# Other constants in the time estimate by which a trace-time scheduler orders a two-layer hybrid transformer

## The chip, the cores and the metric

The kernel runs on one core of a Trainium2 chip. The metric is the device time of one execution in microseconds (us); lower is better. All times come from the hardware profiler or from timed runs.

## The reference

Two layers work on 256 latent tokens and 256 context tokens of width 1024. The second layer gives out the latent tokens alone. In short:

```python
for l in range(DEPTH):                                   # DEPTH = 2
    h_lat = modulate(x, m_lat[0][:, None], m_lat[1][:, None])
    h_ctx = modulate(xc, m_ctx[0], m_ctx[1])
    # token_mixer: one input projection (1024 to N_IN), then
    #   A) differential attention, 4 heads of 2 x 64, rotary positions on latent tokens
    #   B) bidirectional chunked gated delta rule, 4 heads of 128, short convolution on q, k, v
    #   y = (g_a * (ya @ w_pa) + g_b * (yb @ w_pb)) @ w_o
    y_lat, y_ctx = token_mixer(h_lat, h_ctx, ...)
    x = layer_norm(alpha * x + m_lat[2][:, None] * y_lat, ln1_g[l], ln1_b[l])
    # moe_ffn: 16 SwiGLU experts of width 512, router, top-2 inside one of 4 groups
    y = moe_ffn(tokens, router_w, router_b, w_exp1[l], w_exp3[l], w_exp2[l])
    x = layer_norm(alpha * x + m_lat[5][:, None] * y_lat, ln2_g[l], ln2_b[l])
```

All inputs are float32.

## The kernel before, in words

The Python program does not write its instructions in the order in which they run. It describes some eighty strands per layer (generators such as `conv_worker`, `build`, `invert`, `scan`, `attend`, `gates`, `merge`, `out_proj`, `moe_in`, `route`, `expert_up`). Each strand hands operations to a `Scheduler` while the program is being built; the scheduler picks one operation after the other and issues it, so each engine's instruction queue is the order of those picks. On the chip every engine then goes through its queue in that order, and waits on semaphores where an operand is not there yet.

A pick goes by an estimate. Each operation carries a list of (engine, estimated us, function that issues it). `plan` works out when the operation could start: the later of the time at which its engine is free and the time at which its operands are ready plus `LAT` (0.13 us; PE's instructions 0.1 us more). For an operation that ScalarE or VectorE could do, such as `cpy`, it takes the engine with the earlier estimated end, VectorE with a penalty of 1.0 us. A PE operation is counted twice as long where the PE columns counted in the tick before stayed under `COLUMNS`; `emit` counts those columns from the operation's own estimate. `run` then takes, among all strands' next operations, those that could start within 0.05 us of the earliest, and of these the one with the lowest priority number (table `PRIO`, by layer and strand). Strands of negative priority (`moe_in` and `route`) also keep others off an engine: another strand's operation is only taken there if it would end by 0.1 us after the urgent one could start. `emit` books the engine as busy for the estimate, and the result as ready at the same moment.

```python
cand = [(s,) + self.plan(s.q[0]) for s in self.strands if s.q]
...
ok = [c for c in cand if c[0].prio < 0 or c[2] + c[1][1] < due.get(c[1][0], 1e9) + 0.1]
...
    first = min(c[2] for c in ok) + 0.05
    best = min((c for c in ok if c[2] <= first), key=lambda c: c[0].prio)
```

The helpers that record operations hold the constants: `mm` (matmul, line 451 of the trace), `mm_beside` (several experts' matmuls side by side, line 463), `tr` (transpose, line 468), `dve` and `acte` (the formulas for VectorE and ScalarE), `act` (line 480), `cpy` (line 485), `tt` (line 489), `neg` (line 494), `vtr`, `ts` (lines 504 and 506), `affine` (line 511), `stt` (line 518), `vcopy` (line 522), `vset` (line 526), `reduce` (line 529). `mm` and `tr` are PE operations. Because all strands share these helpers, a line of the trace is a kind of operation and not a place in the algorithm; the place is told by the time.

Memory is scheduled too: pages of 128 x 2048 float32 (20 of them), smaller tiles, and 8 PSUM banks are taken and given back by strands, and a table of limits by phase (`LIMITS`) says how many pages the weights may hold. The weights stream in a fixed order (`PLAN`, then each layer's experts), through SP's queue, 1 MB at a time. Weights of the projections are split by `split` into a rounded part and a rest (ScalarE, then VectorE), so that three fast matmuls (`mm3`) replace one full float32 matmul. The experts of rank 2 and higher are loaded by the ranks that the router's counts give, so their loads cannot start before `route` has written `eidi`; those of rank 0 and 1 can be loaded ahead.

Where the steps of the mixer lie in the algorithm: `build` sets up the chunk matrices of the delta rule, `invert` and `double` invert them (small matmuls of 32 x 32, 32 x 64 and 64 x 64), `scan` goes through the chunks, `residual_in` loads the rows that `moe_in` needs (the gate row `gr` by `mod_rows` from `m_dram`), `out_proj` is the last large matmul of a mixer, `moe_in` makes the residual and the norm, `route` the ranking.

Of the kernel before, what the change touches and what calls it, by code (L numbers as in the profile page):

```python
# [12 lines left out]
F32R = mybir.dt.float32r  # L13
BF = mybir.dt.bfloat16
I32 = mybir.dt.int32
AF = mybir.ActivationFunctionType
OP = mybir.AluOpType
# [111 lines left out]
def width(ap):  # L129
    return math.prod(ap.shape[1:])  # L130
# [275 lines left out]
def tile_kernel(ctx, tc, x_in, c_in, ctx_in, cctx_in, mod_w, mod_b, w_in, conv_w, lam_q1, lam_k1, lam_q2,  # L406
# [3 lines left out]
    V, S, G, PE = nc.vector, nc.scalar, nc.gpsimd, nc.tensor  # L410
# [18 lines left out]
    SC = Scheduler(make)  # L429
# [7 lines left out]
    def in_psum(ap):  # L437
        return SC.phys.get(ap.tensor.name, "")[:1] == ("bank",)

    def aps(*xs):  # L440
        return [x for x in xs if x is not None and not isinstance(x, (int, float))]

    def mm(o, a, b, start, stop, beside=False):
        n = max(width(b), 16)
        t = n / 2400 if b.dtype == BF or (b.dtype == F32R and n >= 256) else n / 600
        if beside:
            t = 0.0
        elif b.dtype == F32:
            t = max(t, width(a) / 1200)
        SC.rec([("PE", max(t, 0.022) + 0.003,  # L450
                 lambda: PE.matmul(o, a, b, start=start, stop=stop, skip_group_check=True))], [o], [a, b])  # L451

    def mm3(o, a, b, start, stop):

        mm(o, a[0], b[0], start, False)
        mm(o, a[0], b[1], False, False)
        mm(o, a[1], b[0], False, stop)
# [7 lines left out]

    def tr(o, a, idn=None):
        idn = ident if idn is None else idn
        SC.rec([("PE", 0.11, lambda: PE.transpose(o, a, idn))], [o], [a])  # L468

    def dve(n, ps, r=1.0):  # L470
        return 0.065 + n * 0.00104 * (1.0 if ps else r) + (0.06 if ps else 0.0)

    def acte(n, ps):
        return (0.05 if ps else 0.093) + n * 0.000834

    def act(o, a, f=AF.Copy, bias=0.0, scale=1.0, accum_out=None):
        if f == AF.Copy and (not isinstance(bias, float) or not isinstance(scale, float)):
            f = AF.Identity
        k = {} if accum_out is None else {"accum_out": accum_out}
        SC.rec([("ACT", acte(width(o), in_psum(a)), lambda: S.activation(o, a, f, bias=bias, scale=scale, **k))],  # L480
               aps(o, accum_out), aps(a, bias, scale))

    def cpy(o, a):

        SC.rec([("ACT", acte(width(o), in_psum(a)), lambda: S.activation(o, a, AF.Copy, bias=0.0, scale=1.0)),  # L485
                ("DVE", dve(width(o), in_psum(a), 0.5), lambda: V.tensor_copy(o, a))], [o], [a], pen=1.0)

    def tt(o, a, b, op, e="DVE"):
        opts = [("DVE", dve(width(o), in_psum(a) or in_psum(b)), lambda: V.tensor_tensor(out=o, in0=a, in1=b, op=op)),  # L489
                ("POOL", 0.1 + width(o) * 0.00218, lambda: G.tensor_tensor(out=o, in0=a, in1=b, op=op))]  # L490
        SC.rec({"DVE": opts[:1], "POOL": opts[1:], "ANY": opts}[e], [o], [a, b])

    def neg(o, a):
        SC.rec([("ACT", acte(width(o), in_psum(a)), lambda: S.activation(o, a, AF.Copy, bias=0.0, scale=-1.0)),
                ("DVE", dve(width(o), in_psum(a), 0.5), lambda: V.tensor_scalar(o, a, -1.0, None, op0=OP.mult))],
               [o], [a], pen=1.0)

    def vtr(o, a):
# [3 lines left out]
    def ts(o, a, s1, op0, s2=None, op1=None):  # L502
        if op1 is None:
            f = lambda: V.tensor_scalar(o, a, s1, None, op0=op0)  # L504
        else:
            f = lambda: V.tensor_scalar(o, a, s1, s2, op0=op0, op1=op1)  # L506
        SC.rec([("DVE", dve(width(o), in_psum(a), 0.5), f)], [o], aps(a, s1, s2))

    def affine(o, a, s, b):

        SC.rec([("ACT", acte(width(o), in_psum(a)), lambda: S.activation(o, a, AF.Identity, bias=b, scale=s)),
                ("DVE", dve(width(o), in_psum(a), 0.5),
                 lambda: V.tensor_scalar(o, a, s, b, op0=OP.mult, op1=OP.add))], [o], [a, s, b])

    def stt(o, a, s, b, op0, op1, accum_out=None):
# [3 lines left out]
               aps(o, accum_out), aps(a, s, b))  # L519

    def vcopy(o, a):
        SC.rec([("DVE", dve(width(o), in_psum(a), 0.5), lambda: V.tensor_copy(o, a))], [o], [a])

    def vset(o, x, e="DVE"):
        eng = V if e == "DVE" else G
# [17 lines left out]
    def split(h, lo, a):  # L543

        cpy(h, a)
        tt(lo, a, h.bitcast(F32), OP.subtract)

    def rsqrt(y, a, scale, z):

        ts(a, a, scale, OP.mult, EPS, OP.add)  # L550
        ts(y.bitcast(I32), a.bitcast(I32), -0.5, OP.mult, float(0x5F3759DF), OP.add)
        for _ in range(3):
            tt(z, a, y, OP.mult)
            stt(z, z, -0.5, y, OP.mult, OP.mult)
            stt(y, z, 1.5, y, OP.add, OP.mult)
# [227 lines left out]
    def start():  # L783

        b, w, w2 = yield ("bank", "tiny", "tiny")
        vset(csil, 0.0)
        b0, th = b.v(64), w.v(16)
        tr(b0[:, :48], cr.v(512)[:48, :128], ident[:48, :48])
        act(th, b0[:, :16], AF.Tanh, scale=0.5)
        ts(th, th, 0.5, OP.mult, 0.5, OP.add)  # L790
        tt(csil[:, :, :2].rearrange("p k s -> p s k"), shaped(b0[:, :16], (2, 8)), shaped(th, (2, 8)), OP.mult)
        for l in range(2):
            for kind in range(2):
                c = (l * 2 + kind) * 8
                ts(modb[:, c:c + 8], b0[:, 16 + c:24 + c], float(kind), OP.add)
        SC.free(cr, b, w, w2)
        SC.set(csil_ev)
# [9 lines left out]
    def modulation(ly):  # L807

        yield csil_ev
        for l, i in mod_order:  # L810
# [13 lines left out]
            pt_ = yield "t5"  # L824
            part = pt_.v(512)
            cpy(part, bk)
            SC.free(b)
            b = yield "bank"
# [60 lines left out]
    def vectors(Y):  # L889
# [14 lines left out]
        dma(vv[:, 384:392], dram(a_log, l * 8, [[0, 128], [1, 8]]), "POOL")  # L904
        dma(vv[:, 392:400], dram(dt_bias, l * 8, [[0, 128], [1, 8]]), "POOL")
        tr(b.v(62), vv[:62, 0:128], ident[:62, :62])

        ts(cb_.v(32), b.v(62)[:, :32], 0.5, OP.mult)
# [41 lines left out]
    def make_h(Y, seg):  # L950

        yield Y.hpages_ev
        l, s = Y.l, 1 - seg
        for t in (2 * seg, 2 * seg + 1):
            yield Y.x_ev[t]
        for k in range(0, 8, 2):
            yield mod_ev[l, k // 4]
            yield mod_ev[l, 2 + k // 4]
            tmp, b = yield ("t5", "bank")
            p, h = b.v(2, 256), tmp.v(2, 256)  # L960
            for kk in range(2):
                for i in range(2):
                    tr(p[:, kk, i * 128:(i + 1) * 128],
                       Y.x[seg].v(2, D)[:, i, (k + kk) * 128:(k + kk + 1) * 128])
            for kk in range(2):
                affine(h[:, kk], p[:, kk], modc[:, l, 1, k + kk, s:s + 1], modc[:, l, 0, k + kk, s:s + 1])
            SC.free(b)
            hh, hl = (pg[k // 4].r(4, 512)[:, k % 4:k % 4 + 2, seg * 256:seg * 256 + 256] for pg in (Y.hH, Y.hL))
            split(hh, hl, h)
            SC.free(tmp)  # L970
        SC.set(Y.h_ev[seg])
        if l == 1:
            for i in (2 * seg, 2 * seg + 1):
                yield Y.prev.comb_ev[i]
        SC.free(Y.x[seg])
# [26 lines left out]
    def conv_worker(Y, jobs):  # L1002
# [4 lines left out]
        while jobs:  # L1007
# [22 lines left out]
            if part < 2:  # L1030
                dst = Y.kq(hd)[:, 2 * s0:, 1 - part, :]
                stt(dst, th4, 1.0, a4, OP.add, OP.mult)
                SC.free(b)
                act(a4, dst, AF.Square)
                for t in range(2 * ns):
                    mm(Y.sqs[:, 1 - part, 2 * s0 + t, hd:hd + 1], a4[:, t, :], ones[:, 0:1], True, True)
            else:
                stt(acc_, th_, 1.0, acc_, OP.add, OP.mult)
                SC.free(b)
                tb = yield "bank"  # L1040
                for t in range(4):
                    tr(tb.v(4, 128)[:, t, :], a4[:, t, :])
                cpy(Y.vtok[:, :, hd, :], tb.v(4, 128))
                SC.free(tb)
# [37 lines left out]
    def decay_gates(Y):  # L1082
# [53 lines left out]
        for d in range(2):  # L1136
            vcopy(GC[:, :, d * 4:d * 4 + 4], shaped(bk[:, :32], (2, 4, 4))[:, d])
        vcopy(gv[:, 8, :], bk[:, 32:64])
        SC.free(b)
        act(EGC, GC, AF.Exp)  # L1140
# [91 lines left out]
    def double(Y, groups):  # L1232

        for t, d in groups:
# [46 lines left out]
            for g in (0, 64):  # L1281
                neg(F[g:g + 32, :, g + 32:g + 64], b.v(4, 32)[g:g + 32])
# [25 lines left out]
            if d == 0:  # L1308
                neg(F[lo, :, hi], b.v(4, 64)[lo])
            else:  # L1310
                neg(Um[hi, :, lo], b.v(4, 64)[hi])
                SC.free(ft)
# [1258 lines left out]
```

## Time and profile before

| what | value |
|---|---|
| median of three timed runs | 1615.79 us (1614.47, 1615.79, 1626.0) |
| the profiled execution | 1628.14 us |
| its span, first to last instruction | 1626.0 us |
| mean granted TensorE clock | 0.954 |
| PE busy | 1493.8 us (92%), 9551 matmuls |
| VectorE (DVE) busy | 931.7 us (57%), 2391 instructions |
| ScalarE (ACT) busy | 535.8 us (33%), 950 instructions |
| data moved | 363.17 MB, mean 223 GB/s |

PE is TensorE's matmuls, PEld its weight loads, DVE VectorE, ACT ScalarE, POOL GpSimd, SP the engine that issues most transfers. The busy time of an engine is the time covered by its instructions; an instruction's recorded duration can overlap the next one's. "Idle before <- X" names what ended an engine's idle time. "fp32r" marks tiles written in the rounded format of the fast matmuls; the shapes of matmuls are shown as f32 in either case.

### The profile page before, as it was taken

The numbers are of one execution on the slowest core, as the hardware profiler recorded it, in microseconds if no ns is written. First come the engines' busy times: TensorE is split into PE (matmuls) and PEld (weight loads), VectorE is DVE, ScalarE is ACT, GpSimd is POOL, SyncE is SP. The second block draws the span as 40 slices with busy tenths as digits, with TensorE's granted clock in tenths as the row PEclk, the third lists the DMA queues.
The fourth block names the chain that finished last, engine by engine and source line by source line (L and its number), as shares of the span: only waits on it lengthen the run. The fifth ranks groups of instructions, "written<-read, shape, count | busy, mean of one in ns | idle before, by whom it ended". The sixth has DMA issues, their size and how long they took to land. (4 is left out here: it accounts for less than half of the span.)

```text
span 1626.0 us, 24829 instructions
## 1 busy us (share of the span) xinstructions
PE 1493.8 (92%) x9551; PEld 1017.6 (63%) x9552; DVE 931.7 (57%) x2391; ACT 535.8 (33%) x950; POOL 63.1 (4%) x84
## 2 busy tenths in 40 slices
PE   5999999999999977999999899999999957999974
PEld 2776788756787843465564367788889844454421
DVE  1677945768437586365575966792778666210023
ACT  2533343434331121264553253343554302110110
POOL 1000000000000001111010000000000000000000
PEclk9999999999999997999998999996999977999988
DMA  9415522152336577799998743440055955899994
GB/s 312 158 53 175 160 57 80 50 210 91 117 130 249 190 302 283 277 422 403 417 383 326 260 151 109 156 102 5 28 182 176 312 218 214 304 421 421 420 408 203
DMA packets 147725, 363.17 MB, mean 223 GB/s; under 512 B 27932, under 2 KB 82284, under 8 KB 122256
## 3 DMA queue, kind: packets, MB, share of 16 engines
q1 hardware_dynamic: 139808, 342.91, 56.9%
q0 software_dynamic: 6512, 16.38, 3.0%
q10 hardware_dynamic: 1280, 2.23, 0.4%
q8 instruction: 77, 1.26, 0.3%
q14 instruction: 48, 0.39, 0.1%
HBM read 345.47 MB, written 21.56 MB: 226 GB/s over the span
## 5 line engine op out<-in xcount | busy, mean ns | idle before, releaser
L451 PE MATMUL bank<-page,page 128*128 128x512 f32 (+3 forms) x3776 | 733.7, 349 | 13.5 <-ACT page L485 6.5
L451 PEld LDWEIGHTS bank<-page,page 128*128 128x128 f32 (+2 forms) x3776 | 567.6, 189 | 126.1 <-issue 27.3
L489 DVE TENSOR_TENSOR page<-page,page 128x1024 fp32r<-128x1024 f32 (+3 forms) x219 | 250.8, 1164 | 96.9 <-ACT page L485 94.9
L485 ACT ACTIVATE page<-page 128x1024 fp32r<-128x1024 f32 (+1 forms) x196 | 200.3, 1046 | 122.8 <-PE bank L451 65.8
L463 PE MATMUL bank<-page,t 128*64 128x512 f32 (+2 forms) x736 | 208.9, 607 | 6.8 <-DMA page<-in_w_exp_dram 5.9
L485 ACT ACTIVATE t<-bank 128x512 f32<-128x512 f32 (+5 forms) x168 | 79.8, 480 | 306.7 <-PE bank L468 210.5
L489 DVE TENSOR_TENSOR t<-bank,t 128x512 f32<-128x512 f32 (+3 forms) x63 | 49.6, 792 | 188.0 <-PE bank L463 153.8
L485 ACT ACTIVATE page<-bank 128x512 f32<-128x512 f32 (+2 forms) x127 | 70.2, 557 | 222.1 <-PE bank L451 97.9
L463 PE MATMUL bank<-page,page 128*32 128x512 f32 (+2 forms) x512 | 136.0, 604 | 8.0 <-DMA page<-in_w_exp_dram 7.6
L463 PEld LDWEIGHTS bank<-page,t 128*64 128x64 f32 (+2 forms) x736 | 64.6, 147 | 103.4 <-issue 87.1
L451 PE MATMUL bank<-t,page 32*32 32x16 f32 (+4 forms) x1472 | 117.1, 244 | 2.1 <-DVE t L504 1.8
L451 PEld LDWEIGHTS bank<-t,page 128*128 128x128 f32 (+3 forms) x1472 | 104.9, 160 | 18.9 <-issue 11.3
L468 PE MATMUL bank<-cf,t 128*128 128x128 f32 (+2 forms) x468 | 79.1, 287 | 36.0 <-DVE t L489 25.9
L468 PEld LDWEIGHTS bank<-cf,t 128*128 128x128 f32 (+2 forms) x468 | 54.8, 144 | 70.6 <-DVE t L489 31.8
L463 PEld LDWEIGHTS bank<-page,page 128*32 128x32 f32 (+2 forms) x512 | 47.0, 144 | 81.2 <-issue 67.1
L451 PE MATMUL bank<-page,csil 128*32 128x512 f32 x384 | 68.0, 678 | 17.2 <-DMA page<-in_mod_w_dram 16.5
L451 PE MATMUL bank<-page,t 128*128 128x512 f32 (+2 forms) x392 | 81.4, 346 | 2.1 <-DVE page L489 1.1
L451 PEld LDWEIGHTS bank<-page,t 128*128 128x128 f32 (+1 forms) x392 | 56.0, 185 | 26.4 <-issue 9.2
L518 DVE SCALAR_TENSOR_TENSOR t<-bank,tiny,t 128x508 f32<-128x508 f32 (+3 forms) x96 | 66.5, 700 | 7.5 <-ACT t L480 6.4
L480 ACT ACTIVATE t<-bank,tiny 128x512 f32<-128x512 f32 (+1 forms) x72 | 44.6, 623 | 53.5 <-PE bank L451 27.8
L480 ACT ACTIVATE page<-page 128x512 f32<-128x512 f32 (+2 forms) x44 | 25.6, 588 | 84.1 <-DVE page L489 48.5
L468 PE MATMUL bank<-cf,page 128*128 128x128 f32 (+1 forms) x248 | 41.7, 305 | 9.9 <-DMA page<-h_dram,cd 8.4
(178 smaller groups left out, 1139.7 us busy)
## 6 DMA issues: line engine op xcount, KB each, us to landing
page<-in_w_exp_dram SPq DMA_DIRECT2D x192, 1024.0 KB
page<-in_mod_w_dram SPq DMA_DIRECT2D x48, 1024.0 KB
page<-in_w_in_dram SPq DMA_DIRECT2D x44, 1024.0 KB
page<-in_w_o_dram SPq DMA_DIRECT2D x8, 1024.0 KB
y_dram<-t POOLq DMA_DIRECT2D x6, 1024.0 KB, 8.3
page<-m_dram SPq DMA_DIRECT2D x12, 512.0 KB
page<-y_dram SPq DMA_DIRECT2D x6, 1024.0 KB
page<-in_w_pb_dram SPq DMA_DIRECT2D x4, 1024.0 KB
```

Of the source, the lines that this page charges most:

```text
L451: lambda: PE.matmul(o, a, b, start=start, stop=stop, skip_group_check=True))], [o], [a, b])
L463: PE.matmul(o, a, b, start=start, stop=stop, skip_group_check=True)
L468: SC.rec([("PE", 0.11, lambda: PE.transpose(o, a, idn))], [o], [a])
L480: SC.rec([("ACT", acte(width(o), in_psum(a)), lambda: S.activation(o, a, f, bias=bias, scale=scale, **k))], aps(o, accum_out), aps(a, bias ...
L485: SC.rec([("ACT", acte(width(o), in_psum(a)), lambda: S.activation(o, a, AF.Copy, bias=0.0, scale=1.0)), ("DVE", dve(width(o), in_psum(a), ...
L489: opts = [("DVE", dve(width(o), in_psum(a) or in_psum(b)), lambda: V.tensor_tensor(out=o, in0=a, in1=b, op=op)), ("POOL", 0.1 + width(o) * ...
L518: lambda: V.scalar_tensor_tensor(o, a, s, b, op0=op0, op1=op1, **k))],
```

## The change

Only numbers in the estimate's formulas change; every operation, its operands and the strands stay. `dve(n, ps, r)` has a width n, a flag for an operand in PSUM, and a factor r for forms that run at double rate from SBUF.

```diff
     def mm(o, a, b, start, stop, beside=False):
         n = max(width(b), 16)
-        t = n / 2400 if b.dtype == BF or (b.dtype == F32R and n >= 256) else n / 600
+        t = n / 2250 if b.dtype == BF or (b.dtype == F32R and n >= 256) else n / 600
         if beside:
             t = 0.0
         elif b.dtype == F32:
-            t = max(t, width(a) / 1200)
+            t = max(t, width(a) / 580)
...
-        SC.rec([("PE", 0.11, lambda: PE.transpose(o, a, idn))], [o], [a])
+        SC.rec([("PE", 0.112, lambda: PE.transpose(o, a, idn))], [o], [a])
 
     def dve(n, ps, r=1.0):
-        return 0.065 + n * 0.00104 * (1.0 if ps else r) + (0.06 if ps else 0.0)
+        return 0.15 + n * 0.00104 * (1.0 if ps else r) + (0.02 if ps else 0.0)
 
     def acte(n, ps):
-        return (0.05 if ps else 0.093) + n * 0.000834
+        return (0.175 if ps else 0.21) + n * 0.00082
...
-                ("DVE", dve(width(o), in_psum(a), 0.5), lambda: V.tensor_copy(o, a))], [o], [a], pen=1.0)
+                ("DVE", dve(width(o), in_psum(a), 0.62), lambda: V.tensor_copy(o, a))], [o], [a], pen=1.0)
```

The factor 0.5 becomes 0.62 in the same way in `neg`, `ts` (once for both of its forms), `affine` and `vcopy`. `vset` keeps 0.5, `mm_beside` keeps its formula, and `LAT`, the tick, the column threshold, the priorities, the page limits and the transfer model keep their numbers.

## Rows read from the trace of the kernel before

**Rows 1.** Busy time by stage: stretch, length, busy (x instructions), granted clock, DMA share, GB/s.

```profile
core 0: us, PE busy (x) PEld busy (x) DVE busy (x) ACT busy (x) POOL busy (x), PEclk, DMA share, GB/s
...
40.00:600.00 560.00, 544.66 (x3867) 418.25 (x3860) 364.14 (x944) 199.78 (x386) 12.50 (x18) 0.99 0.42 140
600.00:623.00 23.00, 6.14 (x51) 4.81 (x52) 14.97 (x87) 2.14 (x5) 2.20 (x2) 0.57 0.77 299
623.00:880.00 257.00, 248.07 (x1086) 141.93 (x1086) 144.89 (x279) 114.74 (x145) 27.81 (x29) 0.97 0.92 363
880.00:960.00 80.00, 71.16 (x335) 32.91 (x331) 61.30 (x126) 27.75 (x48) 0.00 (x0) 0.94 0.72 260
960.00:1317.50 357.50, 351.15 (x3032) 299.29 (x3032) 244.08 (x624) 144.72 (x282) 6.71 (x12) 0.95 0.44 146
1317.50:1358.00 40.50, 11.85 (x71) 7.91 (x72) 30.82 (x104) 5.70 (x12) 0.00 (x0) 0.53 0.14 55
1358.00:1605.00 247.00, 230.96 (x990) 99.46 (x992) 50.41 (x168) 32.90 (x56) 6.98 (x7) 0.97 0.95 388
```

**Rows 2.** What PE waited for, whole span: us in total, times, longest us.

```profile
PE bank L468 <- DVE t L489: 25.9, 10, 18.0
...
PE bank L451 <- DVE Mb L489: 13.2, 2, 6.7
...
PE bank L451 <- ACT t L485: 8.0, 12, 2.4
PE bank L451 <- ACT page L485: 6.5, 6, 1.6
...
PE bank L451 <- DVE page L489: 4.2, 8, 0.8
PE bank L451 <- DVE t L504: 3.3, 3, 1.8
PE bank L451 <- ACT page L480: 3.3, 3, 1.6
```

**Rows 3.** The same for PE in the stretch 1317 to 1360.

```profile
PE bank L468 <- DVE t L489: 19.6, 4, 18.0
PE bank L451 <- DVE Mb L489: 6.7, 1, 6.7
PE bank L451 <- DVE t L504: 1.8, 1, 1.8
```

**Rows 4.** The same for PE in the stretch 600 to 640.

```profile
PE bank L451 <- DVE Mb L489: 6.4, 1, 6.4
```

**Rows 5.** Timeline of VectorE, three 512-wide instructions: start us, us, instruction.

```profile
1300.85 0.68 DVE L518 SCALAR_TENSOR_TENSOR t<-page,t 128x512 f32<-128x512 f32 x1
1301.57 0.69 DVE L489 TENSOR_TENSOR page<-page,t 128x512 f32<-128x512 f32 x1
1302.17 0.69 DVE L518 SCALAR_TENSOR_TENSOR page<-page,t 128x512 f32<-128x512 f32 x1
```

**Rows 6.** Timeline of VectorE in a chain of one-column instructions.

```profile
579.52 0.16 DVE L489 TENSOR_TENSOR tiny<-tiny 128x1 f32<-128x1 f32 x1
579.72 0.35 DVE L518 SCALAR_TENSOR_TENSOR tiny<-tiny 128x1 f32<-128x1 f32 x2
```

**Rows 7.** Timeline of ScalarE, two instructions back to back.

```profile
472.58 1.06 ACT L485 ACTIVATE page<-page 128x1024 fp32r<-128x1024 f32 x1 [2.26 <-PE bank L451]
473.55 0.58 ACT L480 ACTIVATE page<-bank 128x512 f32<-128x512 f32 x1
```

**Rows 8.** Timeline of PE: a run of fast matmuls, and a run of narrow float32 ones.

```profile
469.66 12.63 PE L451 MATMUL bank<-page,page 128*128 128x512 f32 x55
...
590.98 0.95 PE L451 MATMUL bank<-cf,t 128*128 128x2 f32 x8
```

**Rows 9.** Busy time and granted clock in the delta-rule stages of layer 0 and layer 1.

```profile
220.00:230.00 10.00, 10.00 (x150) 8.75 (x148) 4.52 (x11) 5.42 (x16) 0.52 (x1) 1.00 0.01 3
...
1100.00:1110.00 10.00, 10.00 (x108) 8.40 (x107) 0.91 (x2) 2.33 (x6) 0.00 (x0) 0.50 0.08 8
```

**Rows 10.** Timeline of PE: the same group of matmuls in both layers.

```profile
208.19 0.68 PE L451 MATMUL bank<-t 64*64 64x64 f32 x8
...
1101.68 1.11 PE L451 MATMUL bank<-t 64*64 64x64 f32 x8
```

**Rows 11.** Timeline of VectorE where the second layer's residual begins.

```profile
1322.50 1.30 DVE L489 TENSOR_TENSOR bank<-bank,page 128x512 f32<-128x512 f32 x2 [10.83 <-DMA page<-m_dram]
```

More of the change, by code (lines that the diff above doesn't have):

```diff
@@ L494, in neg @@
         SC.rec([("ACT", acte(width(o), in_psum(a)), lambda: S.activation(o, a, AF.Copy, bias=0.0, scale=-1.0)),
-                ("DVE", dve(width(o), in_psum(a), 0.5), lambda: V.tensor_scalar(o, a, -1.0, None, op0=OP.mult))],
+                ("DVE", dve(width(o), in_psum(a), 0.62), lambda: V.tensor_scalar(o, a, -1.0, None, op0=OP.mult))],
                [o], [a], pen=1.0)
@@ L506, in ts @@
             f = lambda: V.tensor_scalar(o, a, s1, s2, op0=op0, op1=op1)
-        SC.rec([("DVE", dve(width(o), in_psum(a), 0.5), f)], [o], aps(a, s1, s2))
+        SC.rec([("DVE", dve(width(o), in_psum(a), 0.62), f)], [o], aps(a, s1, s2))
     def affine(o, a, s, b):
         SC.rec([("ACT", acte(width(o), in_psum(a)), lambda: S.activation(o, a, AF.Identity, bias=b, scale=s)),
-                ("DVE", dve(width(o), in_psum(a), 0.5),
+                ("DVE", dve(width(o), in_psum(a), 0.62),
                  lambda: V.tensor_scalar(o, a, s, b, op0=OP.mult, op1=OP.add))], [o], [a, s, b])
@@ L521, in vcopy @@
     def vcopy(o, a):
-        SC.rec([("DVE", dve(width(o), in_psum(a), 0.5), lambda: V.tensor_copy(o, a))], [o], [a])
+        SC.rec([("DVE", dve(width(o), in_psum(a), 0.62), lambda: V.tensor_copy(o, a))], [o], [a])
     def vset(o, x, e="DVE"):
```

## The prediction

> **What bounds the kernel now.** I read the busy times by stage first, to see which engine or queue ends each stage; then what PE waits for; then the timelines, to hold the estimate's constants, old and new, against what the engines really do. The stages [rows 1] show four kinds of stretch. From 40 to 600 and from 960 to 1317.5 (the two mixers) PE is busy 544.7 of 560 us and 351.2 of 357.5 us, at a granted clock of 0.99 and 0.95, with transfers at 0.42 and 0.44 of what the queues can do: PE sets the end there. From 623 to 880 and from 1358 to 1605 (the experts) the transfers run at 0.92 and 0.95, 363 and 388 GB/s: the weights set the end, and their bytes are fixed. From 600 to 623 and from 1317.5 to 1358 (residual, norm, router) PE is nearly idle and VectorE is busy 15.0 of 23 us and 30.8 of 40.5 us: one chain of small operations sets the end, and the expert loads start behind it. From 880 to 960 (between the layers) nothing is full: PE 71.2 of 80 us. So an order of the queues can change four things: the holes of PE in the mixers and between the layers, the chain of the router, the moment at which transfers begin, and the clock.
>
> The holes are small. In the two mixers and between the layers PE is idle 15.3 + 6.4 + 8.8 = 30.5 us [rows 1], 1.9% of the span. Of what PE waited for, the seven largest entries that end at VectorE or ScalarE sum to 64.4 us [rows 2]; 28.1 us of these lie in the second router chain [rows 3] and 6.4 us in the first [rows 4], where PE has no other work. What is left, 64.4 - 28.1 - 6.4 = 29.9 us, is PE standing at an instruction that the estimate put too early, or that was put there for lack of another.
>
> **The change part by part.** No instruction comes or goes, so nothing has a duration of its own to add: every term is one of order. What the new constants do to the scheduler's idea of each engine is worked out first.
>
> *VectorE.* For a 512-wide operation from SBUF the estimate goes from 0.065 + 0.532 = 0.597 us to 0.682 us. The trace records 0.69 us, but the next independent instruction starts 0.60 us after the one before it (1301.57 to 1302.17), and a dependent one 0.72 us after (1300.85 to 1301.57) [rows 5]. The old estimate has 0.597 for the first and, with `LAT`, 0.727 for the second: both right to 0.01 us. The new one has 0.682 and 0.812: each 0.08 to 0.09 us too long. For a one-column operation the chain goes on every 0.20 us [rows 6]; old 0.066 + 0.13 = 0.196, new 0.281. So the recorded duration holds a part that overlaps the next instruction, `LAT` stands for that part already, and the new constants count it twice. *ScalarE.* A 1024-wide operation from SBUF is recorded at 1.06 us and the next starts after 0.97 us [rows 7]; old 0.947, new 1.05: again the record, and not the spacing.
>
> The Trainium skill, page "Perfetto Trace Analysis", section "Optimizing Scalar/DVE Operations", says the same as a rule: the overheads of about 60 ns (VectorE, SBUF) and 93 ns (ScalarE, SBUF) are engine-busy times, and the profiled latency has about twice that, since the half that acknowledges the write overlaps the next instruction. By that rule the new constants are the less true ones for these two engines, and the trace's spacing agrees (0.60 us against a record of 0.69 us); what the rule would make of the time is the second rival below.
>
> *PE.* Here the new numbers are nearer. Fast 512-wide matmuls follow each other every 12.63 / 55 = 0.230 us [rows 8]; old 0.216, new 0.231. Narrow float32 matmuls with 128 weights columns leave two records each, so eight records in 0.95 us are 0.24 us for one [rows 8]; old 0.110, new 0.224. Since `emit` counts columns from the same estimate, narrow matmuls now also count twice the columns, and the scheduler doubles PE's times in fewer places.
>
> Taken together: PE's estimate grows by some 7% in its main kind, VectorE's by 14% at 512 wide, ScalarE's by 11%. The balance between engines hardly moves towards the real one; VectorE and ScalarE look later, relative to PE, than they are. Everything then follows from lists of near ties (0.05 us), so I expect another order almost from the first stages on, of the same kind as before.
>
> The terms, against the profiled execution of 1628.1 us (its span 1626.0 plus 2.1 around it), which stands 12.3 us over the median of 1615.8 us:
>
> 1. Waits of PE on late VectorE and ScalarE results. An estimate that has them late puts other matmuls first, so PE should stand less: between 0 and the whole 29.9 us [rows 2 to 4]. I take half, -15 us, because other work is at hand in a mixer and runs out between the layers.
> 2. Holes made anew. The priorities and page limits stay, but meet other times: strands that fitted behind each other no longer do, weights are split later, a page comes free later. Between 0 and as much again as all holes now, 30.5 us [rows 1]. I take half, +15 us: nothing in the trace says that this order is a better or worse draw than the next.
> 3. Router chains, 23 and 40.5 us. Their operations depend on each other, their strands have negative priority, and little else wants VectorE then; on the chip they go at their own pace whatever the estimate. 0 us. The bounds: the second chain begins at 1322.5 after a wait of 10.83 us for a row from `m_dram` [rows 11], 5 us after PE was done at 1317.5; if SP's queue has that row before the expert weights, -5 us; if it comes a load later or another strand gets in, +5 us.
> 4. Expert stretches, 257 and 247 us: bytes over bandwidth, 0 us, as long as pages for the loads come free in time. PE is busy 248 of 257 us in the first, so this cover is thin there: a later split of weights costs what PE then stands, and is in the upper bound of term 2.
> 5. Clock. From 1100 on, layer 1's delta rule ran at 0.50, the lower of the two levels (1.2 GHz); layer 0's the same work at 1.00 (2.4 GHz) [rows 9], though PE had no idle time before it fell. The same group takes 1.11 us against 0.68 us [rows 10]. The low stretch lasted some 25 us, so it costs about 25 x (1 - 0.68 / 1.11) = 10 us. Another order of small and large matmuls can free layer 1 of it, -10 us, or give it to layer 0 too, +10 us. I take 0.
>
> Sum: -15 + 15 + 0 + 0 + 0 = 0. Against the median that is 1616 us.
>
> **The rivals.** *Slower, about 1640 us.* The chains of the delta rule fall behind. Their steps pass from PE to VectorE or ScalarE and back; each return is now judged 0.085 to 0.12 us later than it is, so one more filler matmul of 0.23 us [rows 8] goes ahead of it in PE's fixed queue. PE is busy meanwhile and nothing is lost, until the projections that serve as filler are used up; from that point the rest of the chain runs alone, with PE waiting at each step. That point is reached where VectorE is already near full, at the end of the chunks in each layer and between the layers. Price: the holes of these three stretches once more, 30.5 us, without the gain of term 1 where PE has nothing else (half of 15), and no new draw, so some 31 - 7 = 24 us: 1616 + 24 = 1640. For it: the double count [rows 5 to 7], and that VectorE is busy 61.3 of 80 us between the layers. Against it: in the mixers VectorE has a third of its time free. By the skill's rule named above this is the side on which the change would fall.
>
> *Faster, about 1595 us.* The waits of term 1 go almost whole (-30 us) and only some new holes come (+9, what the passage between the layers has now): 1616 - 21 = 1595. For it: the PE half of the change is right, and late estimates for the other engines are the safe side for a queue that is PE's. Against it: most of the idle time that could go lies at places where PE had no other instruction ready.
>
> *The change does not do what it says.* The order stays nearly as it is, because most picks are decided by priority and not by time: 1616 us too; it is in the first chance.
>
> **How the numbers follow.** A measurement of this kernel tells about 1% (16 us) from no change; its three runs lie 0.7% apart. Forecast, no change within 1%, 1616 us: 0.45. Slower: 0.35; it gets more than the other side since an order in which PE stands 1.9% has little to give and much to lose. Faster: 0.20. The range takes half of the faster side and most of the slower one, with the clock's 10 us on either end: from 1616 - 21 = 1595 to 1616 + 24 + 10 = 1650. The forecast's own range is 1600 to 1632.
>
> **What would show it.** Right: counts of all groups as before; another order; PE's idle time in the mixers and between the layers still 20 to 45 us; the expert stretches still near 250 us each, with both router chains as long as now. Wrong: a mixer that is more than 20 us shorter or longer; an expert stretch that loses its transfer rate for tens of microseconds; a low clock over a stage that had 1.00; or an order that is the same instruction by instruction.

## The result, and the profile after

The changed kernel takes 1697.8 us (median of 4 runs, 1689.2 to 1708.8), the kernel before 1620.9 us beside it: a ratio of 1.047, 95% interval 1.037 to 1.057, 77 us slower. The forecast was 1616 us, the range ended at 1650. The profiled execution took 1708.8 us, the slowest of the four; its span is 1706.7 us: 80.7 us over the span of before.

PE has the same 9551 matmuls. VectorE and ScalarE have 3341 instructions together as before, but 12 went from ScalarE (950 before) to VectorE (2391 before):

```profile
PE 1530.3 (90%) x9551; PEld 1042.0 (61%) x9552; DVE 938.6 (55%) x2403; ACT 529.3 (31%) x938; POOL 64.1 (4%) x84
```

So what changed is the order and, for these 12, the engine. Two marks cut the span into the same stages in both kernels: the cast of the experts' indices (`eidi`), where a ranking ends, and the last norm of a layer (the second `modc<-modc,lncols`), where layer 1 begins. Each of these lines has the first and the last start in us:

```profile
L522 DVE CAST eidi<-t x2: 174/276/378, 615.8 to 1357.5; 128x16 int32<-128x16 f32 x2
L489 DVE TENSOR_TENSOR modc<-modc,lncols x2: 165/166/168, 925.7 to 926.3; 128x8 f32<-128x8 f32 x2
```

This is before; and after:

```profile
L522 DVE CAST eidi<-t x2: 174/174/174, 657.0 to 1427.7; 128x16 int32<-128x16 f32 x2
L489 DVE TENSOR_TENSOR modc<-modc,lncols x2: 159/160/161, 970.3 to 970.7; 128x8 f32<-128x8 f32 x2
```

| stage | before | after | more |
|---|---|---|---|
| start to ranking 0 | 615.8 | 657.0 | 41.2 |
| ranking 0 to layer 1 | 310.5 | 313.7 | 3.2 |
| layer 1 to ranking 1 | 431.2 | 457.0 | 25.8 |
| ranking 1 to the end | 268.5 | 279.0 | 10.5 |

Whether PE stands or works longer is read from the busy times of these stages, columns as in [rows 1]; before:

```profile
40.00:615.80 575.80, 548.36 (x3907) 420.95 (x3899) 375.36 (x1005) 200.72 (x388) 14.29 (x20) 0.98 0.43 144
926.30:1317.50 391.20, 381.29 (x3214) 320.87 (x3212) 267.09 (x685) 164.84 (x321) 6.71 (x12) 0.94 0.45 147
1317.50:1357.50 40.00, 11.35 (x69) 7.41 (x70) 30.35 (x101) 5.55 (x12) 0.00 (x0) 0.53 0.14 56
1357.50:1377.50 20.00, 19.97 (x75) 10.88 (x75) 13.45 (x64) 3.82 (x6) 0.00 (x0) 0.92 0.89 355
```

and after, the same stages:

```profile
40.00:657.00 617.00, 570.03 (x3913) 435.44 (x3905) 380.83 (x1013) 197.58 (x380) 14.31 (x18) 0.94 0.40 135
970.70:1394.70 424.00, 391.55 (x3214) 331.58 (x3212) 264.30 (x673) 164.80 (x321) 6.71 (x12) 0.91 0.41 136
1394.70:1427.70 33.00, 8.47 (x57) 4.61 (x57) 28.24 (x95) 5.10 (x11) 0.00 (x0) 0.53 0.09 33
1427.70:1447.70 20.00, 16.92 (x62) 11.34 (x63) 12.05 (x65) 2.39 (x4) 0.00 (x0) 0.66 0.66 263
```

Idle time is length less busy time. In layer 0 up to its ranking PE is idle 617.0 - 570.0 = 47.0 us, before 27.4 us: 19.5 us more; and it is busy 21.7 us more for the same matmuls, at a granted clock of 0.94 where it was 0.98. Layer 1 is cut where PE's last matmuls of the mixer end, at 1317.5 in before and at 1394.7 in after. PE's timeline of before:

```profile
1299.82 17.65 PE L451 MATMUL bank<-page,page 128*128 128x256 f32 x146
```

and of after, with VectorE's timeline where the residual begins:

```profile
1379.80 14.88 PE L451 MATMUL bank<-page,page 128*128 128x256 f32 x123
1393.20 1.30 DVE L489 TENSOR_TENSOR bank<-bank,page 128x512 f32<-128x512 f32 x2 [8.24 <-DMA page<-m_dram]
```

Up to that cut, for the same 3214 matmuls, idle goes from 9.9 to 32.4 us, 22.5 us more, and busy from 381.3 to 391.6 us, 10.3 us more. The router chain of layer 1, from the first instruction of the residual to the ranking, is as long as before (35.0 us from 1322.50 [rows 11], 34.5 us from 1393.20). But it begins 1.5 us before PE is done, where it began 5.0 us after; so the layer up to its ranking is 25.8 us longer and not the 32.8 us of its mixer. Behind it the expert loads start slower: 263 GB/s in the first 20 us against 355.

What PE waited for, the rows that answer to [rows 2]:

```profile
PE bank L468 <- DVE t L489: 19.3, 7, 11.5
PE bank L451 <- ACT page L485: 15.8, 10, 6.6
PE bank L451 <- ACT t L485: 15.0, 16, 6.6
...
PE bank L451 <- DVE Mb L489: 12.1, 2, 6.7
PE bank L451 <- DVE t L504: 8.5, 4, 6.5
...
PE bank L451 <- DVE page L489: 7.3, 13, 1.1
...
PE bank L451 <- ACT page L480: 6.2, 4, 2.5
```

The seven entries that summed to 64.4 us sum to 84.2 us. The one that grew most, `ACT page L485` (6.5 to 15.8 us), is in the main the rounding of weights by ScalarE: weights that come late. The longest of `ACT t L485` lies where layer 1 begins (969.69), the longest of `DVE t L504` behind ranking 1 (1430.31).

**The hole of layer 0.** It lies between 120 and 200 us; there PE is busy 66.00 of 80 us, before 79.08 us. Before, then after:

```profile
120.00:200.00 80.00, 79.08 (x481) 56.45 (x480) 66.23 (x194) 29.38 (x47) 2.50 (x5) 1.00 0.54 158
120.00:200.00 80.00, 66.00 (x369) 43.91 (x368) 54.72 (x183) 21.38 (x34) 2.50 (x5) 0.89 0.44 129
```

PE's timeline of after has its longest wait in these rows:

```profile
144.66 1.11 PE L468 MATMUL bank<-cf,t 128*128 128x128 f32 x4 [1.17 <-DVE page L518]
...
157.43 1.74 PE L451 MATMUL bank<-page,page 128*128 128x512 f32 x3 [6.58 <-ACT page L485]
```

ScalarE's timeline tells why the rounding is late:

```profile
156.32 2.00 ACT L485 ACTIVATE page<-page 128x1024 fp32r<-128x1024 f32 x2 [2.74 <-DMA page<-in_w_in_dram]
```

and SP's timeline where that load stood in its queue:

```profile
99.01 23.16 SPq L537 DMA_DIRECT2D page<-in_mod_w_dram  x3
147.53 3.30 SPq L537 DMA_DIRECT2D blk_dram<-page  x7
150.92 0.40 SPq L537 DMA_DIRECT2D page<-in_w_in_dram  x1
```

SP's waits in 100 to 160 have their longest in the first row:

```profile
SPq L537 <- DVE page L518: 27.6, 2, 25.3
SPq L537 <- PE bank L468: 15.1, 1, 15.1
```

SP issued nothing from 122.2 (99.01 + 23.16) to 147.53: it stood at small stores of the block inversion (`blk_dram`), 25.3 us of that for VectorE's line 518, with the weight load behind them. Before, between 100 and 200, SP waited for that line once, for 2.0 us; but it stood 52.4 us there for results of PE, so that SP stands is by itself no proof of harm. Experiment 3 tests it.

**The bare chain of layer 1.** Groups of PE in before, 1090 to 1200, where layer 1's blocks are inverted: among the narrow matmuls lie 129 fast ones (256 wide) of the attention projections.

```profile
L451 PE MATMUL bank<-t,page 128*128 128x128 f32 x216 | 33.8, 308 | 0.3 <-DVE page L489 0.3
L451 PE MATMUL bank<-page,page 128*128 128x256 f32 x129 | 20.7, 300 | 0.2 <-DVE page L489 0.2
```

In after the inversion lies at 1150 to 1270; 2 of that shape are left there. PE's timeline shows the last of them go ahead of it, and PE wait behind them:

```profile
1136.81 12.13 PE L451 MATMUL bank<-page,page 128*128 128x256 f32 x91 [0.77 <-DVE page L489]
1154.24 0.83 PE L451 MATMUL bank<-t,page 32*32 32x16 f32 x44 [5.30 <-DVE t L500]
1156.04 0.90 PE L451 MATMUL bank<-t,t 32*32 32x16 f32 x31 [0.96 <-issue]
```

From 1160 to 1190 the granted clock is 0.50; in before layer 1 fell to 0.50 as well, but layer 0 ran 200 to 280 at 1.00. The two rows of after answer to [rows 9] for layer 0 and layer 1:

```profile
200.00:280.00 80.00, 77.80 (x816) 62.27 (x815) 39.72 (x102) 29.13 (x68) 2.04 (x4) 0.87 0.23 70
...
1160.00:1190.00 30.00, 29.37 (x338) 21.62 (x339) 6.92 (x23) 12.73 (x39) 1.44 (x3) 0.50 0.05 6
```

### The profile page after: what moved, and what is told of

The parts are those of the page before. It is cut to its first block, busy times and chain, and to the rows that moved or that the text cites. A ratio compares the mean times of both kernels' runs of the same rounds, so it can differ in the third digit from the quotient of the medians.

```text
span 1706.7 us, 24811 instructions
## 1 busy us (share of the span) xinstructions
PE 1530.3 (90%) x9551; PEld 1042.0 (61%) x9552; DVE 938.6 (55%) x2403; ACT 529.3 (31%) x938; POOL 64.1 (4%) x84
## 5 line engine op out<-in xcount | busy, mean ns | idle before, releaser
L485 ACT ACTIVATE page<-page 128x1024 fp32r<-128x1024 f32 (+1 forms) x193 | 196.8, 1046 | 158.4 <-PE bank L451 84.5
L463 PE MATMUL bank<-page,t 128*64 128x512 f32 (+2 forms) x736 | 213.7, 619 | 7.7 <-DMA page<-in_w_exp_dram 6.8
L485 ACT ACTIVATE t<-bank 128x512 f32<-128x512 f32 (+5 forms) x165 | 77.7, 479 | 341.7 <-PE bank L468 194.3
L485 ACT ACTIVATE page<-bank 128x512 f32<-128x512 f32 (+2 forms) x127 | 69.9, 554 | 222.3 <-PE bank L451 102.8
L451 PE MATMUL bank<-t,page 32*32 32x16 f32 (+4 forms) x1472 | 127.6, 252 | 11.6 <-DVE t L500 5.5
L451 PEld LDWEIGHTS bank<-t,page 128*128 128x128 f32 (+3 forms) x1472 | 113.0, 167 | 35.6 <-issue 14.2
L468 PE MATMUL bank<-cf,t 128*128 128x128 f32 (+2 forms) x468 | 86.3, 306 | 31.7 <-DVE t L489 19.3
L468 PEld LDWEIGHTS bank<-cf,t 128*128 128x128 f32 (+2 forms) x468 | 60.7, 155 | 65.1 <-issue 22.1
L451 PE MATMUL bank<-page,csil 128*32 128x512 f32 x384 | 73.9, 719 | 24.0 <-DMA page<-in_mod_w_dram 22.9
L451 PEld LDWEIGHTS bank<-page,t 128*128 128x128 f32 (+1 forms) x392 | 61.4, 200 | 24.6 <-issue 8.3
L518 DVE SCALAR_TENSOR_TENSOR page<-page,bank 128x512 f32<-128x512 f32 (+1 forms) x52 | 30.0, 579 | 39.9 <-PE bank L451 34.6
```

Of the source, the lines that this page charges most:

```text
L468: SC.rec([("PE", 0.112, lambda: PE.transpose(o, a, idn))], [o], [a])
L518: lambda: V.scalar_tensor_tensor(o, a, s, b, op0=op0, op1=op1, **k))],
```

## The experiments

**1. Which half of the constants, and whether any shift does it.** Theory A: counting VectorE's and ScalarE's write-back twice does the damage. Theory B: priorities and page limits fit the order that the old numbers give, and any shift breaks it. Theory C: PE's new numbers and the column count that follows from them. Four kernels: PE's three constants alone, VectorE's and ScalarE's alone, and, with all old constants, another `LAT`.

```diff
-        t = n / 2400 if b.dtype == BF or (b.dtype == F32R and n >= 256) else n / 600
+        t = n / 2250 if b.dtype == BF or (b.dtype == F32R and n >= 256) else n / 600
...
-            t = max(t, width(a) / 1200)
+            t = max(t, width(a) / 580)
...
-        SC.rec([("PE", 0.11, lambda: PE.transpose(o, a, idn))], [o], [a])
+        SC.rec([("PE", 0.112, lambda: PE.transpose(o, a, idn))], [o], [a])
```

This is pe_only; vs_only has the rest of the change (`dve`, `acte` and the factor 0.62); lat12 has the line below, lat14 has 0.14 there.

```diff
-    LAT = 0.13
+    LAT = 0.12
```

> Only PE's constants change (2250, 580, 0.112); VectorE's and ScalarE's stay as before. Theory A (VectorE and ScalarE are counted twice, so their constants do the damage): 0.99 to 1.01 of before. Theory B (any shift of the estimate breaks an order that the fixed priorities and page limits fit, whatever its sense): 1.02 to 1.06. Theory C (PE's estimate, with the column count that follows from it, does it): 1.04 to 1.06, as the whole change.

> Only VectorE's and ScalarE's constants change; PE's stay as before. Theory A: 1.04 to 1.06, the whole loss. Theory B: 1.02 to 1.06, but unlike the whole change in where it is lost. Theory C: 0.99 to 1.01.

> A control: the constants of before, and only LAT, the time from an operation's end to the use of its result, 0.12 instead of 0.13 us; no engine is judged slower or faster. Theory A and theory C: 0.99 to 1.01, since 0.01 us is within what the timelines can tell. Theory B: 1.01 to 1.06.

> The same control on the other side, LAT 0.14 us. Theory A and theory C: 0.99 to 1.01. Theory B: 1.01 to 1.06, and lost at other places than with 0.12.

Measured: pe_only 1.032 (1.023 to 1.040), vs_only 1.039 (1.033 to 1.046), lat12 1.018 (1.011 to 1.025), lat14 1.013 (1.005 to 1.020). Each half costs most of the whole, and they don't add; two shifts of 0.01 us that have nothing to do with the change, one either way, cost 1 to 2%. A and C as sole causes fall; B holds, and something beyond the controls is left. By the marks, the time up to ranking 0 is 28.1, 20.5, 15.5 and 10.9 us longer than in before (in the order of the runs above), layer 1 up to its ranking 20.0, 30.8 and 7.8 us longer and, in lat14, 0.8 us shorter: the two mixers lose each time, but for layer 1 in lat14. B had expected vs_only to lose elsewhere than the whole change, which these marks don't show.

**2. The smallest shift.** `LAT = 0.131`. Theory D: the loss grows with the size of the shift.

> A smaller control: LAT 0.131 instead of 0.13 us, one nanosecond, and the constants of before. Theory B (any shift breaks a fitted order): still slower, 1.005 to 1.03, because ties fall the other way and the orders part early. Theory D (the loss grows with the size of the shift, since only a real change of the estimate moves much): 0.995 to 1.005.

Measured 1.011 (1.002 to 1.019). A thousandth of a microsecond gives another order: at 1287 of the 9551 places of PE's queue the trace has another operation, by line and tiles. Its four runs go from 1617.2 to 1642.2 us, the seven of before beside it from 1610.3 to 1638.6 us. The interval takes in both theories' numbers, so it settles little; it leans to B.

**3. Which part of the order.** These kernels don't choose: the scheduler takes its picks (strand and engine) from a recorded list, so two orders can be put together.

```diff
-            cand = [(s,) + self.plan(s.q[0]) for s in self.strands if s.q]
...
-                best = min((c for c in ok if c[2] <= first), key=lambda c: c[0].prio)
+            sid, k = 256 * ORDER[self.at] + ORDER[self.at + 1], ORDER[self.at + 2]
...
+            best = s, o, st
```

after_then_before has after's order up to the first operation of layer 1, before's from there; before_then_after the other way round. after_pool has after's order throughout, with the small transfers of the block inversion (line 537, `blk_dram` and `inv_dram`) issued by POOL and not SP: theory E says that SP standing at them is what costs.

> The picks are read from a list: up to the first operation of the second layer the order of the changed kernel, from there on the order of the kernel before, instruction by instruction. If the loss comes in two parts that don't depend on each other, as the moments of the two rankings say (41 us by the first, then 29 us to the second and 11 us behind it), about 1621 + 42 = 1663 us, ratio 1.02 to 1.03. If the second layer's loss follows from the state that the first one leaves, 1.00 to 1.01 or 1.04 to 1.05.

> The other half: up to the first operation of the second layer the order of the kernel before, from there on that of the changed kernel. Two separate parts: about 1621 + 39 = 1660 us, ratio 1.02 to 1.03, with the same stretch of narrow matmuls without fast ones between in layer 1, at the low clock for a part of it. If the layers hang together: 1.00 to 1.01, or 1.04 to 1.05.

> The order of the changed kernel, read from a list, with the small transfers of the block inversion issued by POOL instead of SP. Theory E (weight loads stand in SP's queue behind transfers that wait for VectorE, 25 us in layer 0, and PE starves for them): 10 to 25 us faster than the changed kernel, ratio 1.03 to 1.04, and the wait of 6.6 us near 151 us is gone. Theory F (the weights are late because their pages come free late, and SP's wait costs nothing): within 5 us of the changed kernel, ratio 1.044 to 1.05.

Measured: 1.024 (1.015 to 1.034), 1.028 (1.020 to 1.037), 1.051 (1.043 to 1.059). The two layers lose separately: 2.4 + 2.8 points are the 4.7 within their intervals. E falls: in after_pool the load of `w_in` went out at 129.71 and not 150.92, PE's wait behind it shrank from 6.58 to 3.38 us, and ranking 0 came at 654.4 and not 657.0; PE was still busy only 68.25 of the 80 us. What comes late there is more than one load. The theory that the text on after_pool calls F (another than the F of experiment 4) expected to be within 5 us of after: the medians are, 1698.6 and 1697.8 us (the ratio, 1.051, lies just over that text's 1.05), but whether pages that come free late are the reason was not tried.

**4. Fast matmuls taken out of the chain.** before's order, in which 122 picks of the attention projections' strands in layer 1 (102 fast 256-wide matmuls with their loads and splits), which lay among the inversion, go ahead of it. Theory F: the missing filler is what layer 1 loses. By the whole run's group (`128x256 f32 x1824 | 246.8`) such a matmul adds 0.135 us, so 102 of them are 14 us of cover.

> The order of before, with one thing moved: in layer 1 the 102 fast 256-wide matmuls of the attention projections that lay among the narrow matmuls of the delta-rule chain, with their splits and loads, go ahead of that chain (122 picks); nothing else moves. Theory F (what layer 1 loses is the missing filler: the fast matmuls are used up before the chain, which then runs alone at the lower clock): the chain's stretch shows PE idle and a granted clock below 0.8 over some 40 us, layer 1 lasts 8 to 20 us longer, ratio 1.005 to 1.012. Theory B (no single move counts for much; the loss is the sum of many small misfits): within 5 us, ratio 0.997 to 1.003.

Measured 1.0157 (1.0122 to 1.0192), 25 us, above what F expected; in the profiled runs layer 1 up to its ranking is 442.2 us long against 431.2 us, 11.0 us more, near the 14 us of work moved. The rows, before and then before_fill_first, tell that PE is idle 5.4 us of these longer (38.6 and 43.9 us) and busy 5.6 us longer:

```profile
926.30:1357.50 431.20, 392.63 (x3283) 328.27 (x3282) 297.44 (x786) 170.39 (x333) 6.71 (x12) 0.90 0.42 139
929.70:1371.90 442.20, 398.26 (x3283) 332.30 (x3282) 298.49 (x785) 170.90 (x333) 6.71 (x12) 0.89 0.40 135
```

PE's timeline shows what the cover had hidden:

```profile
1138.58 1.17 PE L451 MATMUL bank<-t,page 128*128 128x128 f32 x8 [1.19 <-DVE t L518]
1140.60 1.16 PE L451 MATMUL bank<-t,page 128*128 128x128 f32 x8 [0.85 <-DVE t L489]
1143.36 0.44 PE L451 MATMUL bank<-t,page 32*32 32x16 f32 x32 [1.60 <-DVE t L500]
```

and the windows that PE's clock, back at 1.00 from 1130 in before, was lower until 1170:

```profile
1130.00:1140.00 10.00, 8.55 (x57) 7.57 (x56) 4.13 (x14) 1.35 (x3) 0.53 (x1) 0.77 0.01 2
1140.00:1150.00 10.00, 7.46 (x132) 5.79 (x132) 5.70 (x12) 3.40 (x9) 0.00 (x0) 0.74 0.13 37
1150.00:1160.00 10.00, 10.00 (x91) 5.64 (x90) 4.61 (x12) 3.88 (x12) 0.00 (x0) 0.50 0.21 72
```

So F holds for a part of layer 1: one such move makes 11 of the 25.8 us there, and 5.4 of the 18.4 us that PE is idle longer in after up to the ranking (57.0 and 38.6 us). The last section shows that the same order of this layer can differ by 15 us in busy time from one profile to another, which may be why the medians give 25 us and the profiles 11; the idle time is the surer part.

**5. Constants against priorities.** If the pair of constants and priorities counts, other priorities should give back what the new constants lost. refit_prio has after's constants and 49 of the 115 priorities (`PRIO`) chosen anew by trying numbers against the end that the scheduler estimates; old_const_new_prio has those same priorities under before's constants; refit_pe has PE's constants alone and 34 priorities chosen anew in that way. A2: the new constants mislead whatever the priorities. B2: a refit gives back a part, whichever constants.

```diff
-PRIO = {"0ab": 2.106, "0att": 5.949, "0atte": 5.963, "0attend0": 3.942, "0attend1": 2.095, "0attw0": 3.982, "0attw1":
-        1.92, "0build0": 1.465, "0build1": 1.465, "0build2": 1.465, "0build3": 1.465, "0cend": 4.14, "0clear": 4.206,
+PRIO = {"0ab": 1.876, "0att": 5.949, "0atte": 5.475, "0attend0": 3.942, "0attend1": 1.838, "0attw0": 3.982, "0attw1": 6.358,
+        "0build0": 1.465, "0build1": 0.2, "0build2": 1.465, "0build3": 7.138, "0cend": 4.14, "0clear": 4.206, "0comb0": 1.705,
...
```

> After's constants, all of them; 49 of the 115 strand priorities (layer 0's and those of layer 1's mixer) are other numbers, found by trying priorities against the end that the scheduler itself estimates with the new constants. Theory B (the constants are no worse as a description; what was lost is the fit of the priorities, chosen for the old constants): most of the 4.7% comes back, ratio 0.99 to 1.025. Theory A2 (an estimate that counts the engines' write-back twice misleads the scheduler whatever the priorities): ratio 1.035 or more. Between 1.025 and 1.035: both have a part.

> Before's constants with the 49 priorities that refit_prio has: the fourth corner of a square (constants old or new, priorities chosen for the old or the new). Theory B (only the pair of constants and priorities counts): old constants with priorities chosen for the new ones are a misfit too, ratio 1.025 or more. Theory A2 (the constants themselves count: the new ones mislead, the old ones order well): ratio 1.00 to 1.015, well under refit_prio's 1.029. Between: both have a part.

> TensorE's new constants alone (the half that the trace bears out), with VectorE's and ScalarE's old ones, and 34 priorities chosen anew for them in the same way as for refit_prio (the same kinds of strands, the experts of layer 0 included). Theory A2 (the loss that a refit can't bring back comes from the late VectorE and ScalarE): the 3.15% of pe_only goes nearly whole, ratio 0.995 to 1.01. Theory B2 (a refit made with the estimate alone brings back a part, whichever constants): ratio 1.012 to 1.03.

| ratio | before's priorities | the 49 others |
|---|---|---|
| old constants | 1 | 1.0195 (1.0141 to 1.0248) |
| new constants | 1.047 (1.037 to 1.057) | 1.0289 (1.0262 to 1.0316) |

refit_pe measured 1.025 (1.020 to 1.030), pe_only 1.032 (1.023 to 1.040): in B2's range and far from A2's, but the two intervals overlap, so that this refit gave anything back is not shown. With before's priorities the constants cost 4.7 points; with the others, chosen for the new constants, the new ones cost 0.9 points more than the old. So most of the loss belongs to the pair, as B says. The 0.9 points are no more than a shift of 0.01 us costs (experiment 1), so that the constants by themselves cost anything, as A2 says, is not shown. refit_prio and old_const_new_prio both lie in the range where their texts gave both theories a part: a refit gave back 1.8 of the 4.7 points, and neither set of priorities tried came near before. Where it came back is told by the marks: refit_prio's ranking 0 lies at 633.8 (18.0 us late and not 41.2), and its layer 1 takes 436.8 us (5.6 us more and not 25.8).

**6. Where layer 0 loses.** after's order for the first 800, 1200 or 2000 picks of 10,665, then before's. Theory G: the hole of 120 to 200 us. Theory H: the narrow matmuls from 220 us on, at the lower clock.

> After's order for the first 800 picks (of 10665), then before's. The ranking of layer 0 lies at 616 in before and at 657 in after. Theory G (the hole of 120 to 200 us with its late weights costs layer 0 most) and theory H (the narrow matmuls of the block inversion from 220 us on, at the lower clock, cost most) both expect little here: ranking at 614 to 622, ratio within 1.005.

> After's order for the first 1200 picks, then before's. Theory G: the hole is in it, the ranking at 630 to 642, ratio 1.009 to 1.016. Theory H: the ranking at 616 to 626, ratio under 1.006.

> After's order for the first 2000 picks, then before's. Theory G: as with 1200 picks within 5 us. Theory H: the granted clock falls to 0.50 between 220 and 260 as in after and stays 1.00 in the kernel with 1200 picks; the ranking lies 10 us or more later than with 1200 picks, at 636 to 650.

Measured 1.001 (0.998 to 1.005), 1.017 (1.011 to 1.024), 1.013 (1.006 to 1.021); rankings at 623.3, 652.2 and 644.9. The stretch 120 to 200 in after_first_800 has PE busy 78.20 us, in the other two:

```profile
120.00:200.00 80.00, 67.55 (x373) 44.48 (x372) 55.26 (x189) 21.42 (x34) 2.50 (x5) 0.89 0.43 127
```

(1200), and with 2000 picks, with the stretch behind it:

```profile
120.00:200.00 80.00, 67.93 (x369) 44.01 (x368) 54.81 (x183) 21.40 (x34) 2.50 (x5) 0.85 0.44 130
200.00:280.00 80.00, 77.04 (x939) 63.03 (x938) 43.89 (x108) 33.34 (x79) 2.04 (x4) 1.00 0.25 76
```

The loss comes in behind pick 800, and the hole with it; with 2000 picks the clock of 200 to 280 did not fall, and most of the loss is there all the same: G holds and H falls. With 2000 picks the ranking is 29.1 us late, of the 41.2. Of these, 79.08 - 67.93 = 11.2 us are idle time in the hole; for the clock there, 0.85 where it was 1.00, an estimate is 9 us more: the lower level counts 0.50, so its share is twice what the mean lacks to 1.00, 2 x 0.15 x 80 = 24 us, of which 1 - 0.68 / 1.11 = 0.39 [rows 10] is lost. With 1200 it missed G's numbers, by 10 us, and its ranking lies 7.3 us behind that with 2000 picks, where G had at most 5: that kernel's seam lies at the hole, and SP there waits another 45.2 us for VectorE's line 489. So what picks 1200 to 2000 add can't be read from these two. The ranking with 800 picks, 623.3, is 1.3 us later than both theories had it; the ratio there tells that an order from a list costs nothing of itself that these runs can tell.

## Why the prediction was wrong

**What held.** The matmuls are as before, and all but 12 operations keep their engine; the order is another from early on; the router chain of layer 1 keeps its length (term 3, 35.0 and 34.5 us), and it begins earlier against PE, which is the gain of term 3's lower bound. The estimate's arithmetic, by which the new numbers for VectorE and ScalarE are 0.08 us too long, agrees with the spacing [rows 5 to 7]; that this is what cost time is not shown. By what the prediction drew from the Trainium skill, page "Perfetto Trace Analysis", section "Optimizing Scalar/DVE Operations", the change would fall on the slower side, and in direction the runs agree; but PE's constants alone, which that rule does not touch, cost 3.2 points. "The change does not do what it says" fell.

**Term 1** (-15 us, at worst 0) had the wrong sign: the waits on VectorE and ScalarE grew by 84.2 - 64.4 = 19.8 us. Judging those engines late was to make PE stand less; the scheduler then took loads and projections in another order, and the results that PE stood at were split weights and chain steps that were late in truth. These waits are a part of the idle time under term 2, not an addition to it.

**Term 2** (+15 us, at most 30.5) is the first step that failed: "between 0 and as much again as all holes now", and "nothing in the trace says that this order is a better or worse draw than the next". In the two mixers PE's holes grew by 19.5 + 22.5 = 42.0 us. The holes that an order has are no bound for those of another; what its cover hides is nearer to one. For layer 1 that could have been priced from before: the fast matmuls among the inversion, 20.7 us by their group, of which some 14 us moved ahead cost 11 us in the profile and 25 us in the medians. And of the sixteen other kernels run here, the changed one among them, none was faster than before, one was equal (after_first_800), and the rest lost 1.1 to 5.1%. Seven of them have their order from a list; the nine that the scheduler ordered itself lost 1.1 to 4.7%. By these runs before is a far better draw than the next, and terms 1 and 2 as equal halves were the wrong middle.

**Term 4** had the right worry: "this cover is thin". Ranking 1 to the end is 10.5 us longer and the loads start at 263 GB/s; PE is idle 3.3 us and busy 7.2 us more there. Which wait does this was not tried by itself.

**Term 5** (0, between -10 and +10) is the second step that failed, by its size. Over the whole span PE is busy 1530.3 - 1493.8 = 36.5 us more for the same matmuls and idle 44.2 us more. An estimate by the term's own price: a mean granted clock of 0.954 in before is 2 x 0.046 x 1626.0 = 150 us at the lower of the two levels, one of 0.925 in after 2 x 0.075 x 1706.7 = 256 us; 106 us more, of which 0.39 are 41 us. So the clock can account for all of the 36.5 us. That it does is not shown, since the ends of matmuls are modelled.

**The slower rival** had layer 1's mechanism, as far as experiment 4 shows it: fast matmuls used up, then the chain alone. Its price, 24 us for all three stretches, was spent by layer 1 alone (25.8 us). Layer 0's loss, in which PE stands at weights that are rounded late, was in no rival; weights that are split later stood only as a remark under terms 2 and 4.

**What stays open.** Why the weights of the 120 to 200 us hole are late beyond the one load that after_pool brought forward; and how the last 8 to 12 us of layer 0 behind pick 2000 come about.

## What to carry to other kernels

A greedy scheduler's constants and its priorities are one set of numbers: a constant that is truer by itself can cost several per cent (PE's alone cost 3.2), and priorities chosen anew by the same estimate gave back a part at most; a shift of 0.01 us that means nothing can cost 1 to 2%, so control a change with such a shift before reading a meaning into it. To bound what a reordering can lose, don't count the holes that are there; find the chains that depend step by step, and price the independent work that now lies among them, at about its own length for whatever goes elsewhere (one run here: 14 us moved, 11 us lost in the profile, 25 us in the medians). Compare two orders by PE's idle time before its busy time, which the clock moves. Hold an estimate's constant against the spacing of instructions and not against their recorded duration; that this makes an order faster, no run here shows.

## What the hardware showed unexpectedly

The granted clock is not fixed by the order. The kernels after and after_first_2000 issue the same matmuls from 206 us on, with the same times to 0.07 us up to the group at 222; then the one fell to half speed and the other not. PE's timeline of after:

```profile
222.14 0.41 PE L468 MATMUL bank<-cf,page 64*64 64x64 f32 x4
...
224.24 1.11 PE L451 MATMUL bank<-t 64*64 64x64 f32 x8
```

and of after_first_2000:

```profile
222.07 0.41 PE L468 MATMUL bank<-cf,page 64*64 64x64 f32 x4
...
223.49 0.68 PE L451 MATMUL bank<-t 64*64 64x64 f32 x8
```

The groups are those of [rows 10], at the same two durations. after_then_before, with the same order, had 0.68 us there too, and its ranking 0 lies at 653.3 and not 657.0. So the same stretch can go either way in one profile or another; whether the chip that ran it has a part is not shown.

Layer 1 shows what this can be worth. Five profiles have before's order there: before, after_then_before, and after_first_800, _1200 and _2000. From layer 1 to ranking 1 they take 431.2, 429.7, 416.5, 429.6 and 428.4 us. PE is idle 38.2 to 38.9 us in each, and busy 378.3 to 392.6 us for the same 3283 matmuls. The shortest, after_first_800, at a granted clock of 0.95 (before's row, at 0.90, stands in experiment 4):

```profile
935.20:1351.70 416.50, 378.33 (x3283) 317.53 (x3282) 297.30 (x785) 170.00 (x333) 6.72 (x12) 0.95 0.43 144
```

So the clock of one profile, and PE's busy time with it, is no proof of what an order does to it; the idle time came back to within a microsecond.
